# Where branch B of a streaming encoder keeps sigmoid(-z): in PSUM over the scores, or in SBUF under the products

## The chip, the cores and the metric

The kernel runs on one core of a Trainium2 chip. A core has five engines that run side by side, each through its own list of instructions in order: TensorE (PE, matrix products into PSUM; PEld is its loading of weights), VectorE (DVE), ScalarE (ACT, functions such as the sigmoid), GpSimd (POOL) and SyncE (SP, which issues the DMAs). PSUM is a small memory of eight banks that receives TensorE's results; SBUF is the large working memory. Engines wait for each other by semaphores. The metric is the device time of one execution in microseconds (us).

## The reference

One layer of an encoder with two attention branches runs over a prompt of 2048 positions and over 8 running streams of 16 new positions each, with 512 cached ones. Each half projects its inputs, runs both branches, gates them, merges them and projects once more. The change concerns branch B alone, stick-breaking attention with 8 heads of 64:

```python
def stick_breaking_attention(q, k, v, qpos, kpos):
    z = jnp.einsum('bqhd,bkhd->bhqk', q, k,
                   preferred_element_type=jnp.float32) * (HEAD_DIM_B ** -0.5)
    mask = kpos[None, :] < qpos[:, None]
    log_1m = jnp.where(mask, jax.nn.log_sigmoid(-z), 0.0)
    log_a = jax.nn.log_sigmoid(z) + lax.cumsum(log_1m, axis=3, reverse=True) - log_1m
    a = jnp.where(mask, jnp.exp(log_a), 0.0)
    o = jnp.einsum('bhqk,bkhd->bqhd', a, v, preferred_element_type=jnp.float32)
    return o.astype(v.dtype)
```

So the weight of a key is sigmoid(z) of that key times the product of sigmoid(-z) over all later keys. The kernel forms those products without logarithms: a running product from the last key to the first.

## The kernel before

**Units.** The work over the prompt is cut into 8 units: one head of branch A (differential attention, a softmax) or two heads of branch B, in turn, so that units 1, 3, 5 and 7 are of branch B. A unit goes through 16 tiles of 128 query positions, and first a tile of the 128 sample positions, which only gets projected there. Tile t looks at t + 1 blocks of 128 keys, so a unit's late tiles are its long ones. After the eight units a last stage (from about 1800 us on) merges the branches, projects, and beside that runs the sample positions' attention against the caches (`sample`).

**The order of the work.** Each step of the main loop lists three streams: pieces of the projections of tiles ahead (`project`, `transpose_qk`, led by `LEAD` = 5 tiles, into the next unit too), the scores of this tile (`scores`), and the products with the values for the tile two steps back (`pv`, `PV_LAG` = 2). `interleave` merges them by their estimated costs. The program is then ordered on each engine by a scheduler with a timeline of its own, so that what stands where is settled when the kernel is built; on the chip every engine goes through its list in order.

**Branch B's step, by lines.** For one head and a chunk of up to 512 keys (`chunk`):
- L639, L640 (and L643 with the mask, on the diagonal chunk): matmuls write the scores z into a PSUM bank of the ring `ps_s`, which has three banks. f16 high and low halves are multiplied, hence two matmuls.
- `evacuate`, L562 and L563 (shown as L119, the helper that issues activations): ScalarE writes sigmoid(z) into the SBUF buffer `sc_p`, then sigmoid(-z) over the scores in the same PSUM bank.
- `stick`, L616: VectorE runs a scan (`TENSOR_TENSOR_SCAN`) over the chunk from its last key to its first: each element is the one before it times sigmoid(-z), plus zero. It reads PSUM and a column of zeros that is broadcast along the chunk (`zero_t`, SBUF), and writes `sc_n` in SBUF. It starts from the first element of the chunk to the right, or from 2 to the power 14 at the row's end; L615 copies that element where it lies in another buffer. The bank is free for the next scores when the scan is through.
- `stick_weights`, L622: when all chunks of a segment of up to 8 blocks are scanned, GpSimd multiplies `sc_p` by `sc_n`, shifted by one element.
- `turn`, L572 and L573: ScalarE writes the f16 high half of the weights into `sc_n` (whose scan is used up by then), VectorE the low half; a transposing DMA (L580, on SP's queue) moves both into `wt`.
- `pv_block`, L700 and L701: TensorE multiplies `wt` with the values.

`sc_p` and `sc_n` are rings of `SC_BUFS` = 6 buffers each, one of each kind for a segment; `wt` has 5.

**What else the engines do meanwhile.** Projections fill the two banks of `ps_mm` (L428); ScalarE and VectorE split the results into f16 halves (L290, L295; the query at L462, L463), which read PSUM in branch B and, for the rotated queries and keys of branch A, SBUF (`rot`, which GpSimd makes at L469, L471 and L474). TensorE transposes them into the one bank of `ps_t` (L517, L521), and VectorE copies that out in B's units (L531 for k, L532 for qst). The same bank serves the gates' matmuls (L504), which ScalarE copies out (L507). L663 and L683 apply the SiLU gate.

Of the kernel before, what the change touches and what calls it, by code (L numbers as in the profile page):

```python
# [20 lines left out]
AF = mybir.ActivationFunctionType  # L21
# [4 lines left out]
P = 128  # L26
# [83 lines left out]
def layer_kernel(ctx: ExitStack, tc: tile.TileContext, a: dict):  # L110
    nc = tc.nc
    V, S, G, T = nc.vector, nc.scalar, nc.gpsimd, nc.tensor
# [4 lines left out]
    def act(**kw):  # L117

        i = S.activation(**kw)  # L119
        if last_table[0] is not None:  # L120
            tc.add_manual_dep(i.ins, last_table[0].ins.name, NOSYNC, reason="table order")
        last_table[0] = i
        return i
# [63 lines left out]
    def bank(tag, dt=F32):  # L187
        return ps.tile([P, 512 if dt == F32 else 1024], dt, tag=tag, name=f"ps_{tag}", bufs=BANKS[tag])
# [16 lines left out]
    zero_t = con.tile([P, 1], F32, name="zero_t")  # L205
# [330 lines left out]
    def new_job(U, t, c, nb, pool=None):  # L536

        segs = [(0, nb)] if t == NT else [(lo, min(lo + SEG, nb)) for lo in range(0, nb, SEG)]
        return dict(U=U, t=t, c=c, pool=pool, segs=[dict(lo=lo, hi=hi) for lo, hi in segs])

    def buffers(job, seg):
        if "p" not in seg:
            for x in "pn":
                if job["t"] == NT:
                    seg[x] = job["pool"].tile([P, 5 * P], F32, tag="dsc", name="dsc", bufs=4)
                else:
                    seg[x] = scp.tile([P, SEG * P + 4], F32, tag=x, name="sc_" + x, bufs=SC_BUFS)

    def evacuate(job, seg, c, p, lo, n, sc_pos, sc_neg, ch):

        buffers(job, seg)
        if job["U"]["kind"] == 0:
            if "mx" not in job:
                job["mx"] = tiny.tile([P, 2, 4], F32, tag="mx", name="mx")
                job["nch"] = 0
            job["nch"] = max(job["nch"], ch + 1)
            dst = seg[("p", "n")[c]]
            V.tensor_scalar(out=dst[:, lo : lo + n], in0=p[:, 0:n], scalar1=sc_pos, scalar2=None,  # L558
                            op0=ALU.mult, op1=ALU.max, accum_out=job["mx"][:, c, ch : ch + 1])
        else:  # L560

            act(out=seg["p"][:, lo : lo + n], in_=p[:, 0:n], func=AF.Sigmoid, scale=sc_pos)  # L562
            act(out=p[:, 0:n], in_=p[:, 0:n], func=AF.Sigmoid, scale=sc_neg)  # L563

    def turn(job, seg, scale=None):

# [36 lines left out]
            V.scalar_tensor_tensor(out=p, in0=n, scalar=r[:, 2:3], in1=p, op0=ALU.mult, op1=ALU.add)  # L603
            turn(job, seg, r[:, 0:1])

    def stick(seg, later, lo, n, src):

        nk = (seg["hi"] - seg["lo"]) * P
        dst = seg["n"]
        if lo + n == nk and later is None:  # L610
            first = 2.0 ** STICK
        else:
            first = dst[:, lo + n : lo + n + 1]
            if lo + n == nk:
                V.tensor_copy(out=first, in_=later["n"][:, 0:1])  # L615
        V.tensor_tensor_scan(out=dst[:, lo : lo + n][:, ::-1], data0=src[:, 0:n][:, ::-1], data1=zero_t[:, 0:1].to_broadcast([P, n]),  # L616
                             initial=first, op0=ALU.mult, op1=ALU.add)

    def stick_weights(job, seg, later):
        m = (seg["hi"] - seg["lo"]) * P - (later is None)  # L620
        p, n = seg["p"], seg["n"]
        G.tensor_tensor(out=p[:, 0:m], in0=p[:, 0:m], in1=n[:, 1 : m + 1], op=ALU.mult)  # L622
        turn(job, seg)

    def scores(U, t, jobs):

        sc, kind = U["sc"], U["kind"]
        nch = t // 4 + 1
        own = [new_job(U, t, c, t + 1) for c in range(1 + kind)]
        jobs += own  # L630

        def chunk(c, ch):
            job = own[c if kind == 1 else 0]
            seg = job["segs"][ch * 4 // SEG]
            n = 512 if ch < t // 4 else (t % 4 + 1) * P
            p = bank("s")
            qst, kk = U["q", t], U["k"][ch]
            diag = ch == t // 4
            T.matmul(p[:, 0:n], qst[:, c, :], kk[:, c, 0:n], start=True, stop=False)  # L639
            T.matmul(p[:, 0:n], qst[:, 2 + c, :], kk[:, c, 0:n], start=False, stop=not diag)  # L640
            if diag:
                m = mask_a if kind == 0 else mask_b
                T.matmul(p[:, n - m.shape[1] : n], idb, m, start=False, stop=True)  # L643
            evacuate(job, seg, c, p, ch * 512 - seg["lo"] * P, n, sc[:, 3:4], sc[:, 4:5], ch)
            if kind == 0:
                if diag and c == 1:
                    softmax_pair(job)
                return
            i = job["segs"].index(seg)
            later = job["segs"][i + 1] if i + 1 < len(job["segs"]) else None  # L650
            stick(seg, later, ch * 512 - seg["lo"] * P, n, p)
            if ch * 4 == seg["lo"]:
                if later is not None:
                    stick_weights(job, later, None)
                if i == 0:
                    stick_weights(job, seg, later)

        def silu():

            z = silu_z[t % len(rings)]  # L660
            sg = stg.tile([P, 256], F32, tag="r2", name="r2", bufs=1)[:, 0:P]
            act(out=sg, in_=z, func=AF.Sigmoid)
            V.tensor_tensor(out=z, in0=z, in1=sg, op=ALU.mult)  # L663

        order = [(c, ch) for ch in range(nch) for c in range(2)] if kind == 0 else \
                [(c, ch) for c in range(2) for ch in reversed(range(nch))]
        return ([(0.1, silu)] if kind == 1 else []) + [(2.0 if ch < t // 4 else (t % 4 + 1) / 2, lambda c=c, ch=ch: chunk(c, ch)) for c, ch in order]

    def natural(U, t, po, pool=stg):
# [52 lines left out]
    def sample(U, dec, qpad, cs):  # L722
# [33 lines left out]
        def scores_all():  # L756

            box["jobs"] = [new_job(U, t, c, 5, dec) for c in range(heads)]
            qsam, kn = box["s"][:, 0:4, :], box["s"][:, 4:6, :]
            mask = mask_as if kind == 0 else mask_bs  # L760
            pn = bank("s")
            for c in range(2):
                p = pn[:, c * P : (c + 1) * P]
                T.matmul(p, qsam[:, c, :], kn[:, c, 0:P], start=True, stop=False)
                T.matmul(p, qsam[:, 2 + c, :], kn[:, c, 0:P], start=False, stop=False)
                T.matmul(p, idb, mask, start=False, stop=True)
            for c in range(2):
                pc = bank("s")
                for b in range(2):
                    for f in range(2):  # L770
                        for i in range(4):
                            T.matmul(pc[i * 32 : i * 32 + 32, :], qpad[:, f * 2 + c, 2 * i + b, :], box["k", i][:, b * 4 : b * 4 + 4, c, :],
                                     start=(b == 0 and f == 0), stop=(b == 1 and f == 1))
                job = box["jobs"][c % heads]
                seg = job["segs"][0]
                evacuate(job, seg, c, pn[:, c * P : (c + 1) * P], 512, P, sc[:, 3:4], sc[:, 4:5], 1)
                evacuate(job, seg, c, pc, 0, 512, box["f"][:, 0:1], box["f"][:, 1:2], 0)
                if kind == 1:
                    stick(seg, None, 512, P, pn[:, c * P : (c + 1) * P])
                    stick(seg, None, 0, 512, pc)  # L780
                    stick_weights(job, seg, None)
            if kind == 0:
                softmax_pair(box["jobs"][0])
# [39 lines left out]
        steps = [[] for _ in range(13)]  # L823
        steps[4] += [one(queries)]
        steps[6] += [one(scores_all)]
        for i in range(4):
            steps[1 + i] += [one(keys, i)]
# [596 lines left out]
```

## Time and profile before

| what | us |
| --- | --- |
| median of three runs | 2347.12 |
| the three runs | 2343.01, 2347.12, 2352.80 |
| the profiled execution, in all | 2352.01 |
| its span, first to last instruction | 2350.2 |
| TensorE busy | 2124.9 (90%) |
| VectorE busy | 1725.1 (73%) |
| ScalarE busy | 1644.4 (70%) |
| GpSimd busy | 705.0 (30%) |

The profile is of one execution. Busy time counts an instruction from its start to its end, whether it computes or is held up on the way. Waits are given with the instruction that ended them: "PE ps_s L639 <- DVE sc_n L616" is a matmul of line 639 into `ps_s` that stood until the scan of line 616 was through. A group of instructions is told by line, engine, operation, output<-inputs and shape. Line numbers are those of the kernel before.

### The profile page before, as it was taken

Reading aid. Unit: us, or ns where it says so; the run is one execution under the profiler, and the core shown is the slowest. Engines: PE = TensorE matmul, PEld = TensorE weight load, DVE = VectorE, ACT = ScalarE, POOL = GpSimd, SP = SyncE. Lnnn points to the kernel's source line nnn. Section 1 sums busy time; section 2 is a strip of 40 time slices with the busy share of each in tenths; the row PEclk is TensorE's granted clock in tenths of the full one; section 3 lists DMA queues with packets and bytes.
Section 4 is the critical chain, followed back from the end, with each engine's and each line's share of the span. In section 5 each row is a group of like instructions: output and inputs, shape, how many; then the busy total and the mean of one; then the engine's idle time right before and its main releaser. Section 6 shows DMA issues by size and latency. Waiting matters only on the chain. (4 is left out here: it accounts for less than half of the span.)

```text
span 2350.2 us, 42700 instructions
## 1 busy us (share of the span) xinstructions
PE 2124.9 (90%) x15272; PEld 1144.5 (49%) x15272; DVE 1725.1 (73%) x3652; ACT 1644.4 (70%) x3260; POOL 705.0 (30%) x610
## 2 busy tenths in 40 slices
PE   5898899998999999899999979998996879988998
PEld 3554454444555445445545545554553344544443
DVE  4848866779875667978667797877688877777663
ACT  4557878787886778878677777866777656665541
POOL 1533012446300334731033474103335111221111
PEclk8999899999999999999999999999996989999999
DMA  9766759887895988867577787766687999999531
GB/s 334 252 203 177 165 127 263 180 188 163 207 227 131 213 199 189 175 175 191 139 188 175 186 171 185 192 146 149 142 175 162 288 238 250 237 249 243 157 103 48
DMA packets 834357, 445.34 MB, mean 189 GB/s; under 512 B 537210, under 2 KB 777130, under 8 KB 833632
## 3 DMA queue, kind: packets, MB, share of 16 engines
q1 hardware_dynamic: 833196, 442.24, 76.5%
q8 instruction: 119, 1.95, 0.3%
q14 instruction: 94, 0.77, 0.1%
q10 hardware_dynamic: 948, 0.39, 0.1%
HBM read 245.60 MB, written 69.24 MB: 134 GB/s over the span
## 5 line engine op out<-in xcount | busy, mean ns | idle before, releaser
L622 POOL TENSOR_TENSOR sc_p<-sc_p,sc_n 128x127 f32<-128x127 f32 (+7 forms) x192 | 314.2, 1640 | 834.8 <-DVE sc_n L616 812.5
L428 PE MATMUL ps_mm<-wb,hs 128*128 128x512 f16 x1632 | 412.1, 380 | 5.1 <-DMA hs<-hT_d 3.0
L428 PEld LDWEIGHTS <-hs 128*128 128x128 f16 x3120 | 275.8, 99 | 264.5 <-issue 14.8
L428 PE MATMUL ps_mm<-wa,hs 128*128 128x512 f16 x1488 | 377.7, 384 | 9.0 <-DVE qbuf L463 3.8
L616 DVE TENSOR_TENSOR_SCAN sc_n<-ps_s,sc_n,zero_t 128x512 f32<-128x512 f32 x192 | 245.5, 1279 | 80.8 <-ACT ps_s L119 77.5
L639 PE MATMUL ps_s<-k,qst 128*128 128x512 f16 (+3 forms) x640 | 227.5, 356 | 37.2 <-DVE sc_n L616 25.8
L573 DVE TENSOR_TENSOR sc_n<-sc_p,sc_n 128x128 f16<-128x128 f32 (+7 forms) x192 | 211.5, 1106 | 51.8 <-ACT sc_n L572 51.3
L504 PEld LDWEIGHTS <-hs 128*128 128x128 f16 x1632 | 155.6, 98 | 181.4 <-DVE qst L532 5.5
L119 ACT ACTIVATE sc_p<-ps_s,usc 128x512 f32<-128x512 f32 (+3 forms) x320 | 204.3, 638 | 35.3 <-PE ps_s L640 27.9
L640 PE MATMUL ps_s<-k,qst 128*128 128x512 f16 (+3 forms) x640 | 227.1, 356 | 0.0
L572 ACT CAST sc_n<-sc_p 128x128 f16<-128x128 f32 (+7 forms) x192 | 154.9, 811 | 78.9 <-POOL sc_p L622 76.0
L700 PE MATMUL ps_o<-v,wt 128*128 128x128 f16 x1088 | 172.2, 226 | 35.1 <-DMA wt<-sc_n 35.1
L119 ACT ACTIVATE ps_s<-ps_s,usc 128x512 f32<-128x512 f32 (+3 forms) x328 | 199.4, 608 | 0.0
L504 PE MATMUL ps_t<-wb,hs 128*128 128x512 f16 x816 | 192.9, 380 | 2.5 <-DVE qst L532 2.2
L504 PE MATMUL ps_t<-wa,hs 128*128 128x512 f16 x816 | 192.3, 381 | 3.1 <-DVE qst L532 2.2
L1341 PE MATMUL ps_o<-wo,wb 128*128 128x512 f16 x816 | 189.2, 386 | 4.0 <-ACT wb L1163 4.0
L701 PE MATMUL ps_o<-v,wt 128*128 128x64 f16 x1088 | 158.3, 198 | 0.0
L700 PEld LDWEIGHTS <-wt 128*128 128x128 f16 x1088 | 105.6, 101 | 100.1 <-DMA wt<-sc_n 46.4
L558 DVE TENSOR_SCALAR_CACHE_REDUCE sc_n<-ps_s,usc 128x512 f32<-128x512 f32 (+3 forms) x160 | 106.5, 666 | 42.2 <-PE ps_s L640 22.9
L616 DVE TENSOR_TENSOR_SCAN sc_n<-ps_s,zero_t 128x128 f32<-128x128 f32 (+3 forms) x128 | 104.2, 815 | 41.0 <-ACT ps_s L119 38.0
L558 DVE TENSOR_SCALAR_CACHE_REDUCE sc_p<-ps_s,usc 128x512 f32<-128x512 f32 (+3 forms) x160 | 106.4, 665 | 35.6 <-PE ps_s L640 26.1
L701 PEld LDWEIGHTS <-wt 128*128 128x128 f16 x1088 | 103.4, 101 | 54.5 <-issue 1.9
(358 smaller groups left out, 4531.3 us busy)
## 6 DMA issues: line engine op xcount, KB each, us to landing
hs<-hT_d SPq DMA_DIRECT2D x130, 512.0 KB, 4.4
g_d<-gt SPq DMA_DIRECT2D x68, 256.0 KB, 4.4
wb<-g_d SPq DMA_DIRECT2D x26, 512.0 KB, 5.7
out_dram<-pr SPq DMA_DIRECT2D x204, 64.0 KB, 2.4
o_d<-o SPq DMA_DIRECT2D x136, 64.0 KB, 2.0
hs<-o_d SPq DMA_DIRECT2D x17, 512.0 KB, 5.1
out_dram<-x SPq DMA_DIRECT2D x17, 512.0 KB, 2.8
wide<-in_w_ada_dram SPq DMA_DIRECT2D x8, 1024.0 KB, 7.8
```

The costliest lines, as they stand in the source:

```text
L119: i = S.activation(**kw)
L428: T.matmul(box["p"], box["h"][:, hi, k, :], U["w"][k][:, wi, :], start=(n == 0), stop=(n == 3 * KT - 1))
L504: T.matmul(box["g"][:, 0:gw], box["h"][:, hi, k, :], U["wg"][k // per][:, k % per, wi, :], start=(j == 0), stop=(j == 3 * KT - 1))
L558: V.tensor_scalar(out=dst[:, lo : lo + n], in0=p[:, 0:n], scalar1=sc_pos, scalar2=None, op0=ALU.mult, op1=ALU.max, accum_out=job["mx"][:, ...
L573: V.tensor_tensor(out=lo, in0=src, in1=hi, op=ALU.subtract)
L616: V.tensor_tensor_scan(out=dst[:, lo : lo + n][:, ::-1], data0=src[:, 0:n][:, ::-1], data1=zero_t[:, 0:1].to_broadcast([P, n]), initial=fi ...
L622: G.tensor_tensor(out=p[:, 0:m], in0=p[:, 0:m], in1=n[:, 1 : m + 1], op=ALU.mult)
L639: T.matmul(p[:, 0:n], qst[:, c, :], kk[:, c, 0:n], start=True, stop=False)
L640: T.matmul(p[:, 0:n], qst[:, 2 + c, :], kk[:, c, 0:n], start=False, stop=not diag)
L700: T.matmul(po[:, c * P : (c + 1) * P], wt[:, wj, :], vt[:, c, :, :], start=first, stop=False)
L701: T.matmul(po[:, c * P : c * P + 64], wt[:, nb + wj, :], vt[:, c, 0, :], start=False, stop=last)
L1341: T.matmul(po, st["y"][:, yi * 8 + k, :], wo[j * 4 + k // 2][:, wi, k % 2, :], start=(n == 0), stop=(n == 3 * KT - 1))
```

## The change

sigmoid(-z) is no longer written over the scores. ScalarE writes it first, into the part of `sc_n` that the scan will fill, and then sigmoid(z) into `sc_p`. The scan reads `sc_n` and writes it in place. It no longer gets the PSUM tile, so the bank is released by the second sigmoid. The sample positions' attention, which uses the same three functions, changes with it. In the changed kernel all lines behind the scan stand one line lower.

```diff
@@ evacuate
+            act(out=seg["n"][:, lo : lo + n], in_=p[:, 0:n], func=AF.Sigmoid, scale=sc_neg)
             act(out=seg["p"][:, lo : lo + n], in_=p[:, 0:n], func=AF.Sigmoid, scale=sc_pos)
-            act(out=p[:, 0:n], in_=p[:, 0:n], func=AF.Sigmoid, scale=sc_neg)
@@ stick
-    def stick(seg, later, lo, n, src):
+    def stick(seg, later, lo, n):
...
-        V.tensor_tensor_scan(out=dst[:, lo : lo + n][:, ::-1], data0=src[:, 0:n][:, ::-1], data1=zero_t[:, 0:1].to_broadcast([P, n]),
+        x = dst[:, lo : lo + n][:, ::-1]
+        V.tensor_tensor_scan(out=x, data0=x, data1=zero_t[:, 0:1].to_broadcast([P, n]),
                              initial=first, op0=ALU.mult, op1=ALU.add)
@@ chunk
-            stick(seg, later, ch * 512 - seg["lo"] * P, n, p)
+            stick(seg, later, ch * 512 - seg["lo"] * P, n)
@@ sample
-                    stick(seg, None, 512, P, pn[:, c * P : (c + 1) * P])
-                    stick(seg, None, 0, 512, pc)
+                    stick(seg, None, 512, P)
+                    stick(seg, None, 0, 512)
```

## The prediction

> **What bounds the kernel now.** I read the busy totals first, then the waits of TensorE, then four stretches of the branch-B units, then the rows of the scan and of the instructions that resemble the changed scan.
>
> ```profile
> span 2350.2 us, 42700 instructions
> ...
> PE 2124.9 (90%) x15272; PEld 1144.5 (49%) x15272; DVE 1725.1 (73%) x3652; ACT 1644.4 (70%) x3260; POOL 705.0 (30%) x610
> ```
>
> Over the whole span TensorE is the bound, idle for 225 us. The change touches only branch B. The waits, over the span, tell how the scan and TensorE hang together (columns: total us, times, longest):
>
> ```profile
> DVE sc_n L616 <- ACT ps_s L119: 115.5, 114, 5.8
> PE ps_o L700 <- DMA wt<-sc_n: 35.1, 24, 5.2
> PE ps_s L639 <- DVE sc_n L616: 25.8, 35, 2.1
> PE ps_t L517 <- DVE k L295: 12.1, 11, 2.0
> PE ps_mm L428 <- DVE qbuf L463: 5.6, 3, 3.2
> PE ps_t L504 <- DVE qst L532: 4.4, 3, 2.2
> ```
>
> The third row is what the change can give directly: 25.8 us in which a score matmul waited until a scan had let go of its PSUM bank. To see where that lies, I cut each B unit in two by the number of scans and products: its long tiles at the end (first table, 270 us in all), and the rest, from 330 to 500, 720 to 925, 1150 to 1350 and 1560 to 1740 us (second table, the sum alone, 755 us).
>
> ```profile
> 500.00:575.00 75.00, 62.84 (x531) 35.67 (x530) 70.60 (x105) 62.16 (x120) 52.33 (x40) 0.98 0.87 175
> 925.00:1000.00 75.00, 64.33 (x546) 36.15 (x545) 72.20 (x104) 60.90 (x119) 52.91 (x40) 0.98 0.90 184
> 1350.00:1410.00 60.00, 47.72 (x409) 27.20 (x409) 58.25 (x70) 47.08 (x89) 42.53 (x30) 0.98 0.81 172
> 1740.00:1800.00 60.00, 43.26 (x363) 24.81 (x361) 53.60 (x67) 48.09 (x86) 33.88 (x19) 0.80 0.83 171
> sum 270.00, PE 218.16 PEld 123.83 DVE 254.65 ACT 218.22 POOL 181.65; mean PE 54.54 PEld 30.96 DVE 63.66 ACT 54.56 POOL 45.41
> ```
> ```profile
> sum 755.00, PE 722.37 PEld 379.96 DVE 520.24 ACT 569.80 POOL 239.22; mean PE 180.59 PEld 94.99 DVE 130.06 ACT 142.45 POOL 59.81
> ```
>
> The order in a row is time, TensorE, weight load, VectorE, ScalarE, GpSimd. In the early part TensorE is busy 96% of the time, VectorE 69%, GpSimd 32%. In the late part the bound changes hands: VectorE is busy for 254.65 of 270 us (94%, 15 us idle), TensorE for 218, GpSimd for 182 (67%). The bank waits lie there too; the same row from each of the four late stretches adds to 23.4 of the 25.8 us:
>
> ```profile
> PE ps_s L639 <- DVE sc_n L616: 5.8, 8, 1.1
> ...
> PE ps_s L639 <- DVE sc_n L616: 5.1, 8, 1.6
> ...
> PE ps_s L639 <- DVE sc_n L616: 6.3, 9, 1.0
> ...
> PE ps_s L639 <- DVE sc_n L616: 6.2, 8, 2.1
> ```
>
> So what decides is what the change does to VectorE's time while GpSimd is busy.
>
> **The change, part by part.** No instruction, matmul or DMA is added or removed; 336 pairs of sigmoids and 336 scans get other operands.
>
> (1) The scan's input moves from PSUM to SBUF. Its other tensor input, the zero column, already lies in SBUF, so a scan that had one SBUF input now has two. The trace has no such scan. It has instructions in both forms (columns of the first fence: ns minimum/median/maximum; of the second: start, us taken):
>
> ```profile
> L616 DVE TENSOR_TENSOR_SCAN sc_n<-ps_s,sc_n,zero_t x192: 1265/1282/1285, 353.5 to 1801.2; 128x512 f32<-128x512 f32 x192
> ...
> L463 DVE SCALAR_TENSOR_TENSOR qbuf<-rot,sq,qbuf x68: 320/347/2086, 76.6 to 1503.2; 128x128 f16<-128x128 f32 x68
> L463 DVE SCALAR_TENSOR_TENSOR qbuf<-ps_mm,usc,qbuf x68: 324/345/353, 253.8 to 1751.4; 128x128 f16<-128x128 f32 x68
> ...
> L573 DVE TENSOR_TENSOR sc_n<-sc_p,sc_n x192: 266/1093/3052, 331.5 to 1808.3; 128x1024 f16<-128x1024 f32 x80, 128x128 f16<-128x128 f32 x16, 128x256 f16<-128x256 f32 x16, 128x384 f16<-128x384 f32 x16
> ```
> ```profile
> 937.50 1.35 DVE L573 TENSOR_TENSOR sc_n<-sc_p,sc_n 128x1024 f16<-128x1024 f32 x1 [0.45 <-ACT sc_n L572]
> ...
> 948.00 2.83 DVE L573 TENSOR_TENSOR sc_n<-sc_p,sc_n 128x1024 f16<-128x1024 f32 x1
> ...
> 936.35 0.72 POOL L469 TENSOR_TENSOR rot<-pr,rope 128x256 f32<-128x256 f32 x1
> ...
> 947.97 1.77 POOL L622 TENSOR_TENSOR sc_p<-sc_p,sc_n 128x895 f32<-128x895 f32 x1 [0.69 <-DVE sc_n L616]
> 949.70 1.71 POOL L474 TENSOR_TENSOR rot<-rot,r 128x256 f32<-128x256 f32 x1
> ```
>
> L463 is one instruction in two forms of the same shape. Reading PSUM it never took over 353 ns; reading two tensors of SBUF it took up to 2086. The second fence shows the mechanism: a VectorE instruction with two SBUF inputs, issued 0.03 us behind a GpSimd product, took 2.83 us where the same one took 1.35 us before, and the GpSimd instruction behind that 1.71 us where one of its shape took 0.72: each stood still while the other ran. Today's 512-wide scan stays within 1265 to 1285 ns whatever GpSimd does. I take it that the new scan waits like L463 and L573.
>
> [...]
>
> Price: a scan that starts while GpSimd runs waits on average half a GpSimd instruction. Late part: 67% x half of 181.65 us over 129 instructions = 0.47 us, x 98 scans (25, 25, 20 and 28 in the four stretches, where they are 115.4 us of VectorE) = 46 us. Early part: 32% x half of 239.22 us over 195 instructions = 0.19 us, x 222 scans = 43 us. Lower end: nothing, if the broadcast needs no second read. Upper end: these 89 us all on the path. I take the formula, since L463 and L573 are the nearest rows. Late, VectorE has 15 us left: 46 - 15 = 31 us lengthen the span. Early, 43 us fit into 235 us of idle time; what TensorE feels is its waits for VectorE's other results (the last three rows of the waits, 22 us), which I let grow by busy over idle, (563/192)/(520/235) = 1.32: +7 us. GpSimd's own waits, 43% (115.4 of 270 us) x half of 1.18 us x 129 = 32 us late, fit into its 88 us of idle time there.
>
> (2) By itself the scan costs the same. The two forms of L463 have medians of 347 and 345 ns, so I take 0 for the place of the input; 50 ns either way would be 17 us of VectorE.
>
> [...]
>
> (3) The bank is free after the second sigmoid, about 1.3 us earlier. 25.8 us is the most that this returns. But 23.4 us of it lie where VectorE is full: freed there, TensorE reaches the next result that VectorE owes it sooner (k, qst, the query) and waits there. I credit the other 2.4 us, and keep 25.8 as the far end.
>
> (4) sigmoid(-z) comes first, so that a scan can start one sigmoid earlier; of the 115.5 us that scans wait for ScalarE, this can return most, but VectorE's idle time is no bound early, and late it is already spent above: 0. It does offset the later end of a delayed scan for its product, its cast and its transpose, so I leave the waits on the transposed weights (35.1 us) as they are; without that cover the last scan and product of a group, 0.5 us each later, could add 12 us over the 24 waits.
>
> (5) The sigmoid writes SBUF instead of PSUM:
>
> ```profile
> L119 ACT ACTIVATE sc_p<-ps_s,usc 128x512 f32<-128x512 f32 x224 | 157.6, 703 | 31.8 <-PE ps_s L640 27.9 <-PE ps_s L643 3.4
> L119 ACT ACTIVATE ps_s<-ps_s,usc 128x512 f32<-128x512 f32 x224 | 152.1, 679 | 0.0
> ```
>
> 24 ns x 336 = 8 us of ScalarE, which is 75 to 81% busy: hidden. If that cover went, the sigmoids, casts and projection copies queued behind would pay it.
>
> (6) The products' buffer is claimed by ScalarE instead of by the scan, some 2 us earlier. Six buffers rotate; a late transpose would now stop ScalarE, and with it the next scores. No row shows a scan waiting for one, so 0. SP's queue keeps its transfers; behind a late transpose there stand the loads of the hidden state and the stores. The built program has the same instructions in another order (some products stand ahead of the rope sum on GpSimd); I take 0 within 12 us either way, the price found in (4).
>
> **Sum.** 31 + 7 - 2 = +36 us. The profiled execution took 2352 us in all (span 2350.2): 2388. The median of the runs shown, 2347, is 5 us lower: 2383.
>
> **The rivals.**
> - *The bank wait really goes.* Lock as above, but TensorE uses the freed banks to run ahead through the late part, and VectorE's backlog drains in the next A unit: 36 - 23 = +13, 2360. For it: projections run five tiles ahead. Against: their results pass through VectorE in the same queue.
> - *The scan does not contend* (the change's other side). [...] Then the bank waits go and nothing is paid: -26, 2321; with the scan's earlier start relieving VectorE late, some 10 us less. What decides is the scan's maximum: 1285 ns still, or above 2000. Against it: every two-input row stretches.
> [...]
>
> **How the numbers follow.** Forecast 0.47, bank wait gone 0.18, no contention 0.21, feeding on itself 0.14. A difference under 0.5% (12 us) is what a measurement of this kernel can hardly tell from none. The first and last cases are slower; the second lies at its edge and is shared out 0.05 slower, 0.10 same, 0.03 faster; the third gives 0.18 faster and 0.03 same. With 0.02 of the forecast going to same: faster 0.21, same 0.15, slower 0.64. The forecast's own range is 2362 to 2405. The range for all cases reaches from 2325, about half of the third case left out, to 2425, with the far half of the last one left out.
>
> **What would show it.** Right: the 512-wide scan's row spreads from 1280 to over 2500 ns and its mean rises by some 0.3 us; GpSimd's product gets slower; the bank wait on the scan disappears; in the late stretches VectorE is full and TensorE's waits on k, qst and the query grow. Wrong: scans stay at 1285 ns (third case), or they stretch and the late stretches get no longer (second case). Wrong too if ScalarE shows waits for transposes ahead of its sigmoids.

## The result: 2434.7 us, 3.7% slower

The changed kernel took 2434.73 us (median of four runs, 2431.82 to 2436.67) against 2346.73 for the kernel before on the same chip: a ratio of 1.0371, 95% interval 1.0347 to 1.0396, or 88 us more. The prediction was 2383.

The page of the changed kernel: the span with the busy totals, and from the costliest groups the products on GpSimd, after and then before (busy us, mean ns of one | idle before them).

```profile
span 2434.9 us, 42861 instructions
...
PE 2142.3 (88%) x15272; PEld 1153.5 (47%) x15272; DVE 1846.3 (76%) x3652; ACT 1645.6 (68%) x3260; POOL 762.7 (31%) x610
...
L623 POOL TENSOR_TENSOR sc_p<-sc_p,sc_n 128x127 f32<-128x127 f32 (+7 forms) x192 | 333.3, 1739 | 831.6 <-DVE sc_n L617 546.9
```
```profile
L622 POOL TENSOR_TENSOR sc_p<-sc_p,sc_n 128x127 f32<-128x127 f32 (+7 forms) x192 | 314.2, 1640 | 834.8 <-DVE sc_n L616 812.5
```

With the same work, VectorE is busy 121 us longer, GpSimd 58, TensorE 17, ScalarE 1. The view of one line gives the scans' spread (ns minimum/median/maximum; the counts by shape at its end cover only a part of the instructions), the view of groups by shape the 512-wide ones (busy us, mean ns):

```profile
L617 DVE TENSOR_TENSOR_SCAN sc_n<-sc_n,zero_t x320: 392/1284/3023, 327.4 to 1875.0; 128x512 f32<-128x512 f32 x88, 128x128 f32<-128x128 f32 x24, 128x256 f32<-128x256 f32 x24, 128x384 f32<-128x384 f32 x24
```
```profile
L617 DVE TENSOR_TENSOR_SCAN sc_n<-sc_n,zero_t 128x512 f32<-128x512 f32 x224 | 360.6, 1611 | 60.5 <-ACT sc_n L119 52.3 <-DVE sc_n L615 0.5
```

The 512-wide scan, which never took over 1285 ns, now takes 1611 on average and up to 3023. Summed over the 320 scans of the units, the time above each width's mean in the kernel before (1270, 950, 683 and 411 ns for 512, 384, 256 and 128) is 107 us: 46 in tiles 0 to 11, 61 in tiles 12 to 15.

A stretch of the timeline, at the end of unit 1, shows what that does (start, us taken; GpSimd, VectorE, ScalarE):

```profile
545.54 1.71 POOL L469 TENSOR_TENSOR rot<-pr,rope 128x256 f32<-128x256 f32 x1
547.21 1.65 POOL L471 TENSOR_TENSOR r<-pr,rope 128x256 f32<-128x256 f32 x1
548.93 1.52 POOL L474 TENSOR_TENSOR rot<-rot,r 128x256 f32<-128x256 f32 x1
...
556.74 1.99 POOL L623 TENSOR_TENSOR sc_p<-sc_p,sc_n 128x1023 f32<-128x1023 f32 x1 [3.02 <-ACT v L290]
558.69 1.64 POOL L469 TENSOR_TENSOR rot<-pr,rope 128x256 f32<-128x256 f32 x1
...
546.59 3.35 DVE L617 TENSOR_TENSOR_SCAN sc_n<-sc_n,zero_t 128x512 f32<-128x512 f32 x2
...
551.32 2.08 DVE L463 SCALAR_TENSOR_TENSOR qbuf<-rot,sq,qbuf 128x128 f16<-128x128 f32 x1
...
556.88 2.93 DVE L617 TENSOR_TENSOR_SCAN sc_n<-sc_n,zero_t 128x512 f32<-128x512 f32 x1
...
550.48 0.51 ACT L462 ACTIVATE qbuf<-rot,sq 128x256 f16<-128x256 f32 x1 [3.17 <-POOL rot L474]
```

At 556.74 GpSimd begins a product of 1.99 us. The scan issued at 556.88 takes 2.93 us and ends 1.1 us behind the product's end at 558.73; the rotation that GpSimd starts at 558.69 in turn takes 1.64 us, where the prediction's fence has one of 0.72. Further up the three rotations of one query take 4.9 us, ScalarE waits 3.17 us for them, and VectorE's half of that query, L463, is held up for 2.08.

The waits of TensorE after, over the span (total us, times, longest); the corresponding rows of before stand in the prediction:

```profile
PE ps_o L701 <- DMA wt<-sc_n: 55.1, 25, 7.1
PE ps_t L517 <- DVE k L295: 52.2, 15, 7.2
...
PE ps_t L504 <- DVE qst L532: 10.3, 7, 3.7
...
PE ps_s L640 <- ACT sc_p L119: 8.0, 11, 2.5
```

The wait of a score matmul for a scan (25.8 us) is gone. The waits for the halves of the keys grew from 12.1 to 52.2 us, those for the transposed weights from 35.1 to 55.1, those for `qst` from 4.4 to 10.3.

Where the 85 us of span were added: I cut the spans at the first scan of each B unit, at the 49th (the start of tile 12) and at the end of the 80th and last.

| part, over the four B units (us) | before | after | more |
| --- | --- | --- | --- |
| tiles 0 to 11 | 596 | 631 | 35 |
| tiles 12 to 15 | 323 | 363 | 40 |
| A units between them | 555 | 555 | 0 |
| behind the last scan | 548 | 559 | 11 |

For tiles 12 to 15, the windows with each engine's busy time (time, TensorE, weight load, VectorE, ScalarE, GpSimd, granted clock), before and then after:

```profile
477.00:563.00 86.00, 74.59 (x563) 40.10 (x562) 72.41 (x90) 69.80 (x132) 49.68 (x37) 0.98 0.89 184
903.00:986.00 83.00, 72.33 (x572) 39.44 (x571) 71.92 (x90) 68.33 (x131) 50.79 (x36) 0.99 0.89 189
1319.00:1404.00 85.00, 74.15 (x590) 40.89 (x589) 74.34 (x90) 67.69 (x128) 51.46 (x37) 1.00 0.85 189
1733.00:1802.00 69.00, 50.99 (x409) 28.78 (x408) 61.33 (x76) 56.15 (x97) 36.67 (x22) 0.82 0.78 161
sum 323.00, PE 272.06 PEld 149.20 DVE 280.00 ACT 261.97 POOL 188.61; mean PE 68.01 PEld 37.30 DVE 70.00 ACT 65.49 POOL 47.15
```
```profile
481.00:577.00 96.00, 76.65 (x571) 42.19 (x570) 85.97 (x89) 70.41 (x134) 59.31 (x36) 0.91 0.79 170
925.00:1018.00 93.00, 74.27 (x555) 40.59 (x554) 86.13 (x89) 67.47 (x128) 59.14 (x36) 0.94 0.79 174
1361.00:1454.00 93.00, 77.68 (x572) 42.89 (x571) 86.74 (x90) 68.12 (x130) 60.73 (x36) 0.89 0.79 176
1794.00:1876.00 82.00, 50.17 (x395) 28.72 (x392) 79.08 (x77) 57.89 (x99) 44.06 (x22) 0.77 0.65 136
sum 364.00, PE 278.77 PEld 154.39 DVE 337.91 ACT 263.89 POOL 223.24; mean PE 69.69 PEld 38.60 DVE 84.48 ACT 65.97 POOL 55.81
```

VectorE is busy 58 us longer here, its idle time falls from 43 to 26 us, and the stretch is 41 us longer (the windows are cut at whole microseconds, hence 41 and not 40). The 128 scans alone, by the same windows restricted to their line, went from 147 to 209 us.

### The profile page after: what moved, and what is told of

It reads as the page before. It is cut to its first block, busy times and chain, and to the rows that moved or that the text cites. A ratio compares the mean times of both kernels' runs of the same rounds, so it can differ in the third digit from the quotient of the medians.

```text
span 2434.9 us, 42861 instructions
## 1 busy us (share of the span) xinstructions
PE 2142.3 (88%) x15272; PEld 1153.5 (47%) x15272; DVE 1846.3 (76%) x3652; ACT 1645.6 (68%) x3260; POOL 762.7 (31%) x610
## 5 line engine op out<-in xcount | busy, mean ns | idle before, releaser
L623 POOL TENSOR_TENSOR sc_p<-sc_p,sc_n 128x127 f32<-128x127 f32 (+7 forms) x192 | 333.3, 1739 | 831.6 <-DVE sc_n L617 546.9
L617 DVE TENSOR_TENSOR_SCAN sc_n<-sc_n,zero_t 128x512 f32<-128x512 f32 (+3 forms) x320 | 455.7, 1429 | 85.0 <-ACT sc_n L119 76.4
L428 PE MATMUL ps_mm<-wb,hs 128*128 128x512 f16 x1632 | 417.2, 384 | 6.3 <-DMA hs<-hT_d 5.3
L573 DVE TENSOR_TENSOR sc_n<-sc_p,sc_n 128x128 f16<-128x128 f32 (+7 forms) x192 | 207.2, 1083 | 41.2 <-ACT sc_n L572 41.1
L119 ACT ACTIVATE sc_n<-ps_s,usc 128x512 f32<-128x512 f32 (+3 forms) x320 | 204.6, 639 | 32.3 <-PE ps_s L641 17.7
L701 PE MATMUL ps_o<-v,wt 128*128 128x128 f16 x1088 | 176.8, 231 | 55.4 <-DMA wt<-sc_n 55.1
L701 PEld LDWEIGHTS <-wt 128*128 128x128 f16 x1088 | 110.0, 105 | 123.3 <-DMA wt<-sc_n 66.4
L469 POOL TENSOR_TENSOR rot<-pr,rope 128x256 f32<-128x256 f32 x68 | 71.0, 1044 | 200.1 <-ACT pr L442 163.4
L702 PEld LDWEIGHTS <-wt 128*128 128x128 f16 x1088 | 106.8, 103 | 56.2 <-issue 7.7
L1342 PEld LDWEIGHTS <-wb 128*128 128x128 f16 x816 | 78.8, 99 | 103.0 <-issue 8.1
```

The lines of the kernel that those rows point to most:

```text
L428: T.matmul(box["p"], box["h"][:, hi, k, :], U["w"][k][:, wi, :], start=(n == 0), stop=(n == 3 * KT - 1))
L573: V.tensor_tensor(out=lo, in0=src, in1=hi, op=ALU.subtract)
L617: V.tensor_tensor_scan(out=x, data0=x, data1=zero_t[:, 0:1].to_broadcast([P, n]), initial=first, op0=ALU.mult, op1=ALU.add)
L701: T.matmul(po[:, c * P : (c + 1) * P], wt[:, wj, :], vt[:, c, :, :], start=first, stop=False)
L702: T.matmul(po[:, c * P : c * P + 64], wt[:, nb + wj, :], vt[:, c, 0, :], start=False, stop=last)
L1342: T.matmul(po, st["y"][:, yi * 8 + k, :], wo[j * 4 + k // 2][:, wi, k % 2, :], start=(n == 0), stop=(n == 3 * KT - 1))
```

## The experiments

Ratios are to the kernel before, run beside each experiment, with 95% intervals. "Before" and "after" name the kernel that was edited. What the expectations call the contended port is here the measured hold-up between VectorE's instructions with two SBUF inputs and GpSimd's; what in the chip makes it, no run shows.

### Is it the second SBUF input?

**Scores as second input.** The edit gives the scan of after a PSUM tensor in place of the zero column, and a maximum in place of the sum, so that it no longer forms the running product (the pairs of sigmoids stay as changed):

```diff
-        V.tensor_tensor_scan(out=x, data0=x, data1=zero_t[:, 0:1].to_broadcast([P, n]),
-                             initial=first, op0=ALU.mult, op1=ALU.add)
+        V.tensor_tensor_scan(out=x, data0=x, data1=z[:, 0:n][:, ::-1],   # z: the scores' bank
+                             initial=first, op0=ALU.mult, op1=ALU.max)
```

> The changed kernel, but the scan's second tensor input is the chunk's scores in PSUM, combined with max, instead of the column of zeros in SBUF: it computes something else than the running product, with the same work. sigmoid(-z) still goes to sc_n first and is scanned in place there, and the PSUM bank is again held until the scan is through. Theory of the contended port (a scan with two SBUF inputs and GpSimd's reads shut each other out): the scan now has one SBUF input, so its 512-wide maximum falls from about 3000 to under 1290 ns, and the time returns to that of the kernel before, 2335 to 2360 us, with bank waits on the scan back at some 20 us. Theory of the place (what costs is SBUF itself, the claim on the buffer by ScalarE or the order that the scheduler finds): scans may be short, but the time stays at 2410 us or more.

2348.99 us, 0.9983 (0.9967 to 0.9998). The scan's line:

```profile
L617 DVE TENSOR_TENSOR_SCAN sc_n<-sc_n,ps_s x320: 393/1268/1282, 328.9 to 1800.5; 128x512 f32<-128x512 f32 x88, 128x128 f32<-128x128 f32 x24, 128x256 f32<-128x256 f32 x24, 128x384 f32<-128x384 f32 x24
```

With one SBUF input the maximum is 1282 ns again and the loss is gone, though each pair of sigmoids writes the same buffers in the same order as after. The start value, one element of `sc_n`, does not count as an input of this kind: the scans of before had it beside the zeros, both in SBUF, and never took over 1285 ns.

**Without most of the product.** GpSimd's product over 16 columns only, in before and in after:

```diff
-        G.tensor_tensor(out=p[:, 0:m], in0=p[:, 0:m], in1=n[:, 1 : m + 1], op=ALU.mult)
+        G.tensor_tensor(out=p[:, 0:16], in0=p[:, 0:16], in1=n[:, 1:17], op=ALU.mult)
```

> The kernel before with GpSimd's product cut to the first 16 columns of every segment (the other columns of sc_p keep sigmoid(z), so this leaves most of the product out). It is the control for the next kernel. GpSimd loses some 300 us of work that lies in the B units. Both theories: slightly faster than the kernel before, 2290 to 2345 us, because VectorE's low halves (L573) no longer meet a product.

> The changed kernel with GpSimd's product cut to the first 16 columns in the same way (most of the product is left out). Theory of the contended port: with the products gone the scan meets only the rope and gate instructions on GpSimd; the 88 us between the two kernels shrink to under 25 us, or below nothing, since the bank waits go too. Theory of the place or of the order: the two kernels stay 70 to 100 us apart.

2329.32 us, 0.9899 (0.9879 to 0.9920), and 2331.84, 0.9906 (0.9885 to 0.9927): 2.5 us apart, where the full products put 88 between them. So the scan and GpSimd's product hold each other up (the scan's maximum is 1754 ns in the second of these kernels and 3023 in after; the full product took 1739 ns on average in after and 1640 in before), and the bank's earlier release earns nothing when hardly anything contends (the scans of the second kernel still wait 10 us in sum, for the rotations among others).

**The zero column in PSUM.** The column moves to a bank of its own, taken from the score ring; beside it before and after with two score banks:

```diff
-    BANKS = {"mm": 2, "s": 3, "t": 1, "o": 2}
+    BANKS = {"mm": 2, "s": 2, "t": 1, "o": 2}        # all three
...
-    zero_t = con.tile([P, 1], F32, name="zero_t")
+    zero_t = ps.tile([P, 512], F32, tag="z", name="zero_t", bufs=1)   # the first alone
```

> The changed kernel with nothing altered in the scan's order, place or result, but the column of zeros lies in PSUM: it takes one bank, and the scores' ring gets two banks instead of three. The scan has one SBUF input and the bank is free after the second sigmoid. Theory of the contended port: the scan's 512-wide maximum stays under 1290 ns; the third bank, held one scan shorter than before, is hardly missed: 2335 to 2375 us, and some 70 us under the same kernel with the zeros in SBUF. Were the early release of the bank worth what it looks like in the waits (25 us), it would be below 2340 us.

> The kernel before with two banks for the scores instead of three: the price of a bank where the scan holds it. Expected 2375 to 2440 us, with bank waits on the scan well above 26 us. If it stays within 10 us of three banks, the early release of the bank was worth nothing to begin with.

> The changed kernel with two banks for the scores: the control for the zeros in PSUM, from which it differs by the place of the zeros alone. Theory of the contended port: 2430 to 2460 us, scans up to 3000 ns. Theory of the place: within 15 us of the kernel with the zeros in PSUM.

Zeros in PSUM: 2440.01 us, 1.0357 (1.0337 to 1.0377). After with two banks: 2491.35, 1.0580 (1.0556 to 1.0604). Before with two banks: 2532.66, 1.0756 (1.0736 to 1.0776). All three lie above what was expected: a score bank is worth more than I had thought. The scan's line with the zeros in PSUM, then with the zeros in SBUF and two banks:

```profile
L617 DVE TENSOR_TENSOR_SCAN sc_n<-sc_n,zero_t x320: 390/1268/1282, 347.2 to 1889.5; 128x512 f32<-128x512 f32 x88, 128x128 f32<-128x128 f32 x24, 128x256 f32<-128x256 f32 x24, 128x384 f32<-128x384 f32 x24
```
```profile
L617 DVE TENSOR_TENSOR_SCAN sc_n<-sc_n,zero_t x320: 393/1283/3023, 348.6 to 1941.1; 128x512 f32<-128x512 f32 x88, 128x128 f32<-128x128 f32 x24, 128x256 f32<-128x256 f32 x24, 128x384 f32<-128x384 f32 x24
```

The place of one column of zeros decides whether the scan waits: 51 us between kernels that differ in nothing else, for in the two traces every engine's instructions stand in the same order. Of all the kernels here they are the only two of which that is so. By stretches, its 40 us of scan waits in tiles 0 to 11 cost 9 us, and its 60 us in tiles 12 to 15 cost 43. Without its contention the change is worth 93 us with two banks (2532.66 - 2440.01), most likely by the bank's earlier release; the two programs stand in different orders, so that it isn't separated.

**The same bank from another ring.** With three score banks the room comes from `ps_o`, which goes from two banks to one, in both kernels:

```diff
-    BANKS = {"mm": 2, "s": 3, "t": 1, "o": 2}
+    BANKS = {"mm": 2, "s": 3, "t": 1, "o": 1}        # both; the first also has the zeros in PSUM
```

> The zeros in PSUM again, but their bank is taken from the ring of the output sums (one instead of two), and the scores keep three. If the two rivals of the prediction are settled as the other runs say, the scan costs what it did and the scores' banks come free early: 2330 to 2400 us, depending on what the output's second bank is worth, above all in the last stage, where the final projection uses it.

> The kernel before with one bank for the output sums instead of two: the control for the zeros in PSUM with one output bank (2390 us), from which it differs in where sigmoid(-z) lies and in when the scores' bank comes free, with scans of one SBUF input in both. If the early release of the bank is worth the 25 us that the waits show, this kernel is 2405 to 2420 us; if it is worth nothing with three banks, as with the narrow products, 2380 to 2398 us.

After with the zeros in PSUM: 2390.25 us, 1.0157 (1.0136 to 1.0178). Before: 2390.10, 1.0149 (1.0118 to 1.0180). Freed of contention, the whole change is worth 0 within these intervals. In tiles 12 to 15 TensorE waits 37 us in the kernel before and 39 in the other: 19.1 us at the bank fall to 0, while those for the key halves grow from 2.8 to 14.3 us.

### The order of the two sigmoids

```diff
-            act(out=seg["n"][:, lo : lo + n], in_=p[:, 0:n], func=AF.Sigmoid, scale=sc_neg)
             act(out=seg["p"][:, lo : lo + n], in_=p[:, 0:n], func=AF.Sigmoid, scale=sc_pos)
+            act(out=seg["n"][:, lo : lo + n], in_=p[:, 0:n], func=AF.Sigmoid, scale=sc_neg)
```

> The changed kernel with the two sigmoids in the order of the kernel before: sigmoid(z) first, sigmoid(-z) second, the scan still in place in SBUF. Theory of the contended port: the order of the sigmoids has little to do with it; the scan can start 0.7 us later, so 2425 to 2450 us. Theory of the order (what costs is that scans come earlier and collide with the products of the group before): under 2410 us.

2423.04 us, 1.0300 (1.0274 to 1.0325), below the changed kernel's interval (1.0347 to 1.0396) and between the two cases of the expectation: sigmoid(-z) first costs some 12 us by the medians and 17 by the ratios. The scans wait for 90 us here and for 107 there, which fits, but why the old order makes them wait less is not shown.

### Where it is lost: early and late tiles

The change in some tiles only, the other tiles and the sample positions as before:

```diff
+    def in_sbuf(t):
+        return t < 12              # the second kernel: 12 <= t < NT
...
+        src = dst[:, lo : lo + n] if src is None else src[:, 0:n]   # None where in_sbuf(t)
```

> The change in tiles 0 to 11 of each B unit alone; tiles 12 to 15 and the sample positions as before. The prediction held that the waits there (43 us) are nearly hidden by VectorE's idle time, +7 us: 2350 to 2365 us. If idle time on VectorE does not hide them, the 36 us that the stages with these scans grew by in the changed kernel come back here: 2378 to 2400 us.

> The change in tiles 12 to 15 of each B unit alone. The prediction's term for the late part was +31 us, less 23 us if the banks' early release is a gain: 2360 to 2385 us. From the stages of the changed kernel +38 us: 2385 to 2400 us. If early and late tiles feed each other's waits, the two kernels with one part each add up to clearly less than the 85 us of the whole.

Early tiles alone: 2373.73 us, 1.0096 (1.0072 to 1.0120), +22. Late tiles alone: 2416.09, 1.0273 (1.0250 to 1.0295), +64. Together 86 of the 88, and both cost more than the prediction's terms; early came out between the two cases of its expectation, late above both. That the sums agree is in part chance, for the stretches don't agree. The early change alone adds 24 us to its own tiles, where after adds 35. The late change alone adds 41 to its own tiles (after: 40) and another 25 where its code leaves the work as it was: 5 in the early tiles, 11 in the A units and 9 behind the last scan. Early alone has its instructions in nearly the order of before; late alone stands in quite another. TensorE's waits by cause, summed over the same stretches:

| TensorE waits for (us) | before | after | early alone | late alone |
| --- | --- | --- | --- | --- |
| tiles 0 to 11, all | 32.0 | 53.5 | 47.5 | 34.0 |
| tiles 12 to 15: the scan (bank) | 23.4 | 0 | 24.9 | 0 |
| tiles 12 to 15: the key halves | 12.0 | 49.5 | 11.7 | 39.5 |
| tiles 12 to 15: transposed weights | 14.2 | 26.5 | 15.3 | 27.4 |

What the bank gave back in the late tiles, TensorE spends waiting for the keys of the next A unit, which VectorE splits, and more. In the last B unit there is no next unit, and the transposed weights take that place. The groups by shape of the late kernel show both scans side by side:

```profile
L623 DVE TENSOR_TENSOR_SCAN sc_n<-sc_n,zero_t 128x512 f32<-128x512 f32 x104 | 174.8, 1682 | 15.4 <-ACT sc_n L119 11.3
L623 DVE TENSOR_TENSOR_SCAN sc_n<-ps_s,sc_n,zero_t 128x512 f32<-128x512 f32 x96 | 122.8, 1279 | 50.2 <-ACT ps_s L119 48.8
```

### Is it only VectorE's time?

**A longer scan that holds nobody.** Before, with a reduction of one SBUF input behind each scan, whose result nobody uses; all tiles, then tiles 12 to 15 alone:

```diff
                              initial=first, op0=ALU.mult, op1=ALU.add)
+        junk = tiny.tile([P, 1], F32, tag="jr", name="jr")
+        V.tensor_reduce(out=junk, in_=dst[:, lo : lo + min(n, 256)], axis=AX.X, op=ALU.max)
```

> The kernel before, and behind every scan VectorE takes the maximum over up to 256 of the scanned columns, a result that nobody reads: some 0.33 us more of VectorE for each scan, about what the contended scan loses (108 us in all), with one SBUF input, so that GpSimd isn't held up, and known to the scheduler. Theory of VectorE's time (it is VectorE's added time alone that lengthens the span): 2400 to 2440 us. Theory of the mutual hold-up (GpSimd's later products and delays that the scheduler didn't plan for count as much): 2355 to 2390 us.

> The kernel before with the maximum of up to 256 columns behind the scans of tiles 12 to 15 alone: about 53 us of VectorE at the very place where the change in those tiles alone made scans wait 56 us and lengthened the span by 63 us. If VectorE's time at that place is what counts, 2395 to 2415 us. If half or more of the 63 us comes from the mutual hold-up (rope, query and keys of the next A unit late on GpSimd and VectorE, in lumps that the scheduler did not plan for), 2365 to 2385 us.

All tiles: 2408.50 us, 1.0243 (1.0215 to 1.0272), +57 for 133 us of VectorE, with GpSimd's 1024-wide products at 2104 ns on average (2184 in before). Late tiles: 2386.01, 1.0135 (1.0101 to 1.0168), +32 for 52. The windows' sum over tiles 12 to 15 of the late one:

```profile
sum 348.00, PE 280.23 PEld 155.06 DVE 322.85 ACT 265.05 POOL 179.54; mean PE 70.06 PEld 38.77 DVE 80.71 ACT 66.26 POOL 44.89
```

VectorE +43 us, stretch +25: of such time some 18 us go into its idle time, as in after (58 and 41). Its waits:

```profile
PE ps_s L642 <- DVE sc_n L616: 48.8, 52, 2.6
...
ACT qbuf L462 <- POOL rot L474: 30.3, 23, 3.7
...
PE ps_t L517 <- DVE k L295: 11.6, 12, 1.9
```

Here TensorE stands at the bank, not at the keys, and ScalarE's wait for the rotation stays at before's level (30.3 us against 34.0; 52.2 in after). So a delay of VectorE by itself explains part of the late loss, 32 of 64 us, if the place of the added work and the other order of the program don't matter; the result lies between the two cases of the expectation.

**Shorter products.** Each product of GpSimd in three instructions, with the busy time that this adds: in before, in before with the longer scan, and in after:

```diff
-        G.tensor_tensor(out=p[:, 0:m], in0=p[:, 0:m], in1=n[:, 1 : m + 1], op=ALU.mult)
+        for a, b in ((2 * m // 3, m), (m // 3, 2 * m // 3), (0, m // 3)):
+            G.tensor_tensor(out=p[:, a:b], in0=p[:, a:b], in1=n[:, a + 1 : b + 1], op=ALU.mult)
```

> The kernel before with each of GpSimd's products split into three instructions of a third of the columns: the same work, and by the rows of the products (1024 columns 2.0 us, 127 columns 0.41 us, so 0.18 us fixed) 0.36 us more for each, 69 us of GpSimd in all, against some 58 us that GpSimd loses in the changed kernel. No scan is held up by it. The prediction's step (GpSimd's waits fit into its idle time): 2345 to 2360 us. If GpSimd's delays reach the path through the casts or through the next A unit's rope, keys and query: 2370 to 2395 us.

> Both at once: the maximum behind every scan (133 us of VectorE, +57 us by itself) and the split products. If the two engines' delays add, as a mutual hold-up would have it, 2420 to 2450 us, where the changed kernel lies; if VectorE's time alone counts, 2400 to 2418 us.

> The changed kernel with each product split into three instructions on GpSimd: same work, 69 us more of GpSimd by its fixed costs. If a scan waits for half of whatever GpSimd instruction it meets, as the prediction's formula has it, thirds of a product cut the scans' waits from 107 us to 40 to 60 us and the time falls to 2385 to 2415 us, although GpSimd does more. If instead GpSimd's own delays are what lengthens the span, it rises above 2435 us.

Before: 2359.72 us, 1.0028 (1.0007 to 1.0048). With the longer scan: 2385.78, 1.0141 (1.0111 to 1.0171), less than the longer scan alone (1.0243). After: 2418.19, 1.0287 (1.0258 to 1.0317). The expectations of the last two missed. I had meant the split as a pure delay of GpSimd, and it is none: with the shorter GpSimd instructions VectorE's other two-input work took less time too (L573 is busy 234 us with the longer scan alone, 194 with the split). In after the scans' maximum shows it:

```profile
L617 DVE TENSOR_TENSOR_SCAN sc_n<-sc_n,zero_t x320: 392/1284/1909, 329.9 to 1866.4; 128x512 f32<-128x512 f32 x88, 128x128 f32<-128x128 f32 x24, 128x256 f32<-128x256 f32 x24, 128x384 f32<-128x384 f32 x24
```

The scans' waits fell from 107 to 54 us, but the time by 16 us only. GpSimd is now busy for 943 us (763 in after) and ScalarE waits 169 us for products (129 in after), which is the likely reason. So these runs say that the scan's wait shrank with the length of one GpSimd instruction (its maximum from 3023 to 1909 ns), and nothing on the rest.

**Without the rotation.** The three rotations per tile of branch A left out, in before and in the kernel with the change in tiles 12 to 15:

```diff
-                G.tensor_tensor(out=rot..., in0=x4, ..., op=ALU.mult)
...
+                rot = pr
```

> The kernel before without the rotation of branch A's queries and keys (GpSimd's three instructions a tile, 180 us in all, are left out, and the split reads the projection itself): the control for the next kernel. GpSimd has only products and gates left: 2320 to 2350 us.

> The change in tiles 12 to 15 alone, also without the rotation. Scans still meet products; their waits should fall from 56 us to some 40 us. If the rotation of the next A unit, queued on GpSimd behind products that wait for scans, is how the late waits reach TensorE (through the query and the keys), the distance to the control falls to what VectorE's time alone costs at that place, 32/52 of the waits: 20 to 30 us. If the mutual hold-up costs as much by any other way (casts, or simply delays that the scheduler didn't plan for), it stays near 63/56 of the waits: 40 us or more.

Before: 2355.97 us, 1.0009 (0.9994 to 1.0024), where at least a few us less were expected: leaving out the rotation gains the kernel before nothing (its late tiles are 13 us shorter, its early ones 15 longer). Late: 2388.30, 1.0159 (1.0136 to 1.0182), so the late change costs 32 us without the rotation, between the two cases of the expectation, and 64 with it, though the scans wait as long (54.6 and 56.4 us). The windows' sums for tiles 12 to 15, before without rotation and late without rotation:

```profile
sum 308.00, PE 270.64 PEld 150.50 DVE 269.06 ACT 259.82 POOL 148.40; mean PE 67.66 PEld 37.63 DVE 67.27 ACT 64.95 POOL 37.10
```
```profile
sum 344.00, PE 275.70 PEld 153.30 DVE 320.82 ACT 264.80 POOL 157.29; mean PE 68.93 PEld 38.33 DVE 80.20 ACT 66.20 POOL 39.32
```

VectorE +52 us for +32 us of time is the rate of the longer scan (43 for 32); with the rotation it was +58 for +64. That the other half of the late loss comes through the rotation on GpSimd is not shown, though. By stretches the late tiles grow by 34 us without and 41 with it (8 us apart) and the A units by 2 and 11 (9 apart). The rest of the difference lies in the early tiles (12 us shorter without the rotation, 5 longer with it) and behind the last scan, which the late change doesn't touch. The four programs stand in different orders, and that alone moves such stretches by 10 to 15 us.

## Why the prediction was wrong in size

The direction and the hold-up between the scan and GpSimd's instructions were right, and the size of the waits nearly so; the steps that said what the waits cost were not. Of the 49 us of span that the forecast of 36 lacks, 28 lie in tiles 0 to 11 (35 instead of 7), 9 in tiles 12 to 15 (40 instead of 31) and 11 behind the last scan (no term).

**Step 1, the mechanism: right, and shown.** The scan waits like L463 and L573 (up to 3023 ns; they took up to 2086 and 3052 in before). The zero column counts as an input though it is one element a partition: with two score banks and the column in SBUF the scan's maximum is 3023 ns, with the column in PSUM 1282.

**Step 1, the waits: nearly right.** 0.47 us a scan were forecast late, and 61 us over 128 scans are 0.48; 0.19 early, and 46 over 192 are 0.24. In sum 89 against 107. The late agreement is partly luck, since the prediction's late part is another stretch with 98 scans: on the cut at tile 12 the same formula gives 0.42 late (58% x half of 188.61 us over 132 instructions) and 0.21 early, so the measured waits are some 15% longer.

**Step 1, "31 us lengthen the span" late: mis-sized, 40.** What VectorE's idle time took up was forecast well (15 us; 58 - 41 = 17). But I drew the full part too short: 270 us with 98 scans, where tiles 12 to 15 are 323 us with 128 scans. The other 30 scans were counted as early ones, at the early price and with cover. The pair with two banks, 43 us for 60 us of waits, fits this account.

**Step 1, "early, 43 us fit into 235 us of idle time": failed; in the changed kernel this is the largest error.** The early tiles grew by 35 us, and the change made there alone costs 22, not 7. VectorE was idle for 30% of that stretch before, but TensorE was busy for 95% of it, and idle time averaged over 755 us doesn't help an instruction that is late now. I had let three rows of TensorE's waits for VectorE grow. In these tiles they come to 10 us before and after: the query's halves fell from 5.7 us to 0, `qst` grew from 4.4 to 10.3, and the keys' are nought in both (of their 52.2 us over the span 49.5 lie in the late tiles). What grew are waits for ScalarE's copy of the gates (2.5 to 10.9 us), for the loads of the hidden state (4.5 to 9.8) and for the sigmoid that now frees the bank (0 to 4.3). ScalarE in turn waited 80 us for GpSimd's products there instead of 48. So the waits seem to go from the scan through the product and ScalarE to TensorE, which is argued from these rows and not shown. All of TensorE's waits rose by 21.5 us, from 32.0 to 53.5. The remaining 13 of the 35 us are a longer busy time for about as many matmuls (564 to 577 us), whose cause stays open. With two banks and the same order of instructions the early waits cost only 9 us, so the price depends on the program around them.

**Step 1, "GpSimd's own waits fit into its idle time": doubtful, not settled.** In busy time they do fit (GpSimd 223 of 364 us). But a rotation behind a held-up product can be late, as the timeline shows (1.64 us for one instruction of it, ScalarE waiting 3.17 us for another rotation), and the query and keys of the next unit are made from it. The two runs without the rotation are 32 us nearer to each other than those with it, of which 8 us lie in the late tiles and 9 in the A units; the rest lies where the change isn't.

**Step 2, no other cost of the scan: right.** In the late kernel both kinds stand side by side; the view of its line gives 392 ns for the shortest scan from SBUF, 395 from PSUM:

```profile
L623 DVE TENSOR_TENSOR_SCAN sc_n<-sc_n,zero_t x128: 392/1285/3020, 481.3 to 1859.8; 128x512 f32<-128x512 f32 x104, 128x128 f32<-128x128 f32 x8, 128x256 f32<-128x256 f32 x8, 128x384 f32<-128x384 f32 x8
L623 DVE TENSOR_TENSOR_SCAN sc_n<-ps_s,zero_t x96: 395/815/1224, 329.4 to 1770.4; 128x128 f32<-128x128 f32 x24, 128x256 f32<-128x256 f32 x24, 128x384 f32<-128x384 f32 x24, 128x512 f32<-128x512 f32 x24
```

The two are 3 ns apart.

**Step 3, the bank: right.** With three banks and one SBUF input in both kernels the wait moved to VectorE's other results, the keys among them, as the step said, and the change is worth 0.

**Step 4, the order credited at 0 and the transposed weights left as they are: failed.** The order costs 12 to 17 us, and the waits for transposed weights grew by 20 us, 12 of them in the late tiles. The step named the price of 12 us for a lost cover and then did not take it.

**Steps 5 and 6: as forecast.** ScalarE is busy 1 us longer; a sigmoid of the scores waits for a transpose once, for 0.2 us. That the bank's release now hangs on ScalarE shows as 8 us of waits.

**Unpriced: the tail.** Of the 11 us behind the last scan I had no term, though 16 scans of the sample lie there (they wait 2 us in sum). It stays open whether they are the cause: that part takes 543 to 565 us in the other kernels, with and without the change there.

**The rivals.** "The scan does not contend" and "the bank wait really goes" fell with the first runs. "Feeding on itself" stands for step 1's upper end, all 89 us on the path: 2347 + 89 = 2436, nearly the result. That is roughly what happened, 85 us of span for 107 of waits, but the waits did not feed on themselves: per late scan they were 0.48 us, not much larger than the 0.42 of the simple formula. What made them costly late is what stands behind VectorE, the keys (TensorE's waits there from 12.0 to 49.5 us) and the transposed weights (14.2 to 26.5); early it is open.

## What to carry to other kernels

Count the SBUF inputs of a VectorE instruction, a broadcast constant too, before moving an operand out of PSUM: here the 512-wide scan with two of them took up to 3023 ns beside GpSimd's products, with one never over 1285, and the products went from 1640 to 1739 ns on average. Its waits could be sized to within a fifth (half of a GpSimd instruction times GpSimd's busy share), but they could not be laid into the idle time of a long stretch: on a queue in order, ask which result behind the delayed instruction the busiest engine needs next. A freed buffer was worth nothing here where its engine then waited for something else.

## What had not been expected of the hardware

- The change without its contention is worth 93 us with two score banks and nothing with three.
- Adding work to GpSimd in shorter instructions made the kernel with the longer scan faster (1.0141 against 1.0243) and after too (1.0287 against 1.0371), while before gained nothing (1.0028).
- TensorE's granted clock in the first three late stretches is 0.89 to 0.94 after and 0.98 to 1.00 before, where TensorE is busy for 80 to 84% of the time instead of 87%. Why the clock is lower isn't shown, and what it costs wasn't separated from the waits.
